# Substitution steps of a chunked scan moved one batch behind their loads, two buffers for the scan's loads, and a starting matrix that is loaded

## The chip, the cores and the metric

The kernel runs as one program on one core of a Trainium2 chip. The core has five engines that a trace names: PE (TensorE, the matmuls; PEld is its loading of weights), DVE (VectorE), ACT (ScalarE), POOL (GpSimd) and SP (SyncE, which here only issues DMAs). Each works through its own instructions strictly in order; they meet at semaphores. DMA transfers run beside them, started by an issue instruction on one of the engines' queues. The metric is the device time of one execution in microseconds (us).

## The reference

The reference runs two blocks one after the other. The first (a gated linear recurrence and dilated attention) is not touched. The second normalises and projects its input, feeds four branches (a pool mixer, a differential attention, a bidirectional RWKV scan and gates), merges them and ends with a mixture of experts. The change sits in the RWKV scan, which the reference writes as a step over tokens, 768 of them (256 of context and 512 latent), for two directions and 8 heads of 64:

```
def wkv_step(S, inp):
    r, w, k, v, a, b = inp
    sa = jnp.einsum('dbhvk,dbhk->dbhv', S, a)
    S = S * w[..., None, :] + sa[..., None] * b[..., None, :] + v[..., None] * k[..., None, :]
    return S, jnp.einsum('dbhvk,dbhk->dbhv', S, r)
```

## The kernel before

The scan is done in chunks of 64 tokens: 4 chunks of context and 8 latent ones, in each of two directions d, 24 in all. Two chunks make a batch; the 12 batches n = 0 to 11 alternate between the directions. Each batch has three functions:

- `ph_a`, once for each chunk: loads `kb` (b, k and decay of the chunk, 384 KB, L1133) and `kr`; four scans on DVE make the running sum of the decay, `cs` (L1143, L1145); ACT makes `ep` (L1147) and `em` (L1149), its exponentials with either sign; POOL and DVE scale `kr` by `ep` into the two halves of `AR` (L1153, L1155), POOL copies `dec` from `ep` (L1151), DVE scales b and k by `em` into `BK` (L1157). PE multiplies `BK` and `AR` (`pA`, L1163), DVE masks the product into `AMB` (L1167), and PE and ACT put a transpose of `BK` beside it (`ptb`, L1172, L1175).
- `ph_i`, once for each batch: the 32x32 blocks of `AMB` are stored to DRAM (`atD`, four DMAs, L1184) and loaded back as `LT`, 512 KB, the blocks repeated over partitions (L1187). `Ti`, the starting matrix, is copied from a constant by ACT (L1190). Then come 31 substitution steps of two small DVE instructions each (`Tm`, L1195, and `Ti`, L1197; 372 of each in all), which invert unit triangular blocks. Four DMAs store the result (`ttD`, L1200).
- `ph_b`, run by `run_b` for the batch two back: loads the inverse (`TT`, L1214) and the values (`XV`, `XW`), finishes the inverse with small matmuls `pi` and copies `T1` and `Qs` (L1246, L1247), makes `px` (L1269, copied to `XV` at L1272 and L1273), `pW` (L1283) and `WW` (DVE L1290 and L1292, ACT L1293), and carries the state `SI` over the chunks (`pch`, L1301 to L1313).

Between the batches the program is given other work of the second block, mainly projections with 512 KB weight loads (`wr`, L297; split by `wh` on ACT, L304, and `wl`, L305; matmuls `pf`) and the preparation of queries and keys.

No order is written out by hand. The program is built by a scheduler that simulates the engines with its own model of durations and, from the order of the code, the data and the free buffers, fixes one order for each engine's queue ahead of time. The tags that `w1` gives a tile have a number of buffers (`kb` 1, `ep` 2, `LT` 2, `Ti` 2, `AR` 6, `AMB` 3): an instruction that fills a buffer waits until the readers of what it held before are done, and what stands behind it on its queue waits with it. With one buffer, the load of `kb` for a chunk waits until `BK` of the chunk before has read it.

Of the kernel before, what the change touches and what calls it, by code (L numbers as in the profile page):

```python
# [12 lines left out]
AF = mybir.ActivationFunctionType  # L13
# [26 lines left out]
def _consts():  # L40
    f = np.float32
    groups, off = {g: [] for g in "012345"}, {}
    where = {"bias1": "1", "invf": "1", "cos2": "3", "sin2": "3", "hsel": "5", "hbc": "5",
             "mask": "2", "tinit": "2", "sgn": "2",
             "iota32": "4", "tokid": "4", "tri": "4", "slot": "4", "tokrow": "4"}

    def add(name, a):
        a = np.asarray(a, f)
        a = a.reshape(128, -1)
        g = where.get(name, "0")  # L50
        off[name] = (g, sum(p.shape[1] for p in groups[g]), a.shape[1])
        groups[g].append(a)

    p = np.arange(128)
    add("ident", np.eye(128))
    j = np.arange(512)
    d = p[:, None] - j[None, :] + 384
    n = ((d >= 0) & (d <= 128)).astype(int) + ((d >= 0) & (d % 4 == 0)) + ((d >= 0) & (d % 16 == 0))
    add("bias1", np.where(n > 0, np.log(np.maximum(n, 1).astype(np.float64)), NEG))
    add("invf", np.broadcast_to((10000.0 ** (-np.arange(32) / 32)).astype(f), (128, 32)))  # L60
    sel = np.zeros((128, 2))
    sel[0::32, 0] = 1
    sel[1::32, 1] = 1
    add("sel8", sel)
    add("ones", np.ones((128, 1)))
    add("nhalf", np.full((128, 8), -0.5))
    t = np.arange(512)
    inv16 = (10000.0 ** (-np.arange(16) / 16)).astype(f)
    ar = (t // 64).astype(f)[:, None] * inv16
    ac = (t % 64).astype(f)[:, None] * inv16  # L70
    cr, sr, c_, s_ = (fn(a.astype(np.float64)) for a in (ar, ac) for fn in (np.cos, np.sin))
    add("cos2", np.concatenate([cr, cr, c_, c_], 1).reshape(4, 128, 64).transpose(1, 0, 2))
    add("sin2", np.concatenate([-sr, sr, -s_, s_], 1).reshape(4, 128, 64).transpose(1, 0, 2))
    hs = np.zeros((128, 4, 8))
    hb = np.zeros((128, 4, 128))
    for ft in range(4):
        for e in range(2):
            hs[64 * e:64 * e + 64, ft, 2 * ft + e] = 1
            hb[2 * ft + e, ft, 64 * e:64 * e + 64] = 1
    add("hsel", hs)  # L80
    add("hbc", hb)
    b1 = np.zeros((128, 128))
    b1[:64, :64] = 1
    b1[64:, 64:] = 1
    add("bones", b1)
    add("iota32", np.broadcast_to(np.arange(32), (128, 32)))
    add("slot", np.broadcast_to(np.arange(64), (128, 64)))
    add("tokid", np.arange(512).reshape(4, 128).T)
    add("tokrow", np.broadcast_to(np.arange(512), (128, 512)))
    add("tri", p[:, None] < p[None, :])  # L90
    r = np.arange(64)

    m = np.zeros((128, 2, 2, 128))
    sg = np.ones((128, 2))
    for dd, (lt, le) in enumerate(((r[:, None] < r[None, :], r[:, None] <= r[None, :]),
                                   (r[:, None] > r[None, :], r[:, None] >= r[None, :]))):
        tr = np.concatenate([lt, le], 1)
        for e in range(2):
            m[64 * e:64 * e + 64, dd, e] = -0.5 * tr
            m[64 - 64 * e:128 - 64 * e, dd, e] = tr  # L100
    for e in range(2):
        sg[64 * e:64 * e + 64, e] = -0.5
    add("mask", m)
    add("sgn", sg)
    ti = np.zeros((4, 32, 8, 32))
    for g in range(4):
        for q in range(8):
            ti[g, :, q, 4 * q + g] = 1
    add("tinit", ti)
    return {"cst" + g: np.concatenate(v, 1) for g, v in groups.items()}, off  # L110


_CST, _COFF = _consts()
# [77 lines left out]
def _build(ctx, tc, A, out, dbg, upto):  # L191
    nc = tc.nc
    V, SC, GP, PE, SY = nc.vector, nc.scalar, nc.gpsimd, nc.tensor, nc.sync
# [87 lines left out]
    def cc(name):  # L281
        g, o, w = _COFF[name]
        return csts[g][:, o:o + w]
# [186 lines left out]
    for i in range(4):  # L470
        t = t2("x%d" % i, w=1024, tag="t4")
# [189 lines left out]
    for z, (ft, e) in enumerate(att):  # L661
# [6 lines left out]
        for j in range(4):  # L668
            pt = ps("pT", "aux")
            n = 512 - 128 * j  # L670
# [370 lines left out]
    for f in range(8):  # L1041
        src, g = (ya[f], vv("norm_rec")[:, f:f + 1]) if f < 4 else (yb[f - 4], vv("norm_att")[:, f - 4:f - 3])
# [52 lines left out]
    load_cst("2", cp2)  # L1095
    mask = cc("mask").rearrange("p (d e t) -> p d e t", d=2, e=2)
    sgn = cc("sgn")
    tinit = cc("tinit").rearrange("p (j t) -> p j t", j=8)
    ones64 = cc("ones")[:, 0:1].to_broadcast([128, 64])
    CW = 0.5 * math.exp(-0.5)  # L1100
    atD = [dp.tile([2, 2, 8, 32, 32], F32, name="atD%d" % i) for i in range(4)]
# [6 lines left out]
    def w1(name, shape=(4, 64), bufs=1, dt=F32):  # L1108
        p = rp if name == "AZ" else rpa if name in EARLY else rpb
        return p.tile([128] + list(shape), dt, tag=name, name=name, bufs=bufs)  # L1110
# [10 lines left out]
    for d in range(2):  # L1121
        for e in range(2):
            t = rp.tile([128, 4, 64], F32, name="SI%d%d" % (d, e))
# [5 lines left out]
    def ph_a(d, c, s, AMB):  # L1129

        lat = c >= 4
        kb = w1("kb", (3, 4, 64), 1)
        SY.dma_start(kb, kbD[lat][:, d, c - 4 * lat])  # L1133
        kr = w1("kr", (2, 4, 64), 2)
        SY.dma_start(kr[:, 0], kkD[:, c])
        if lat:
            SY.dma_start(kr[:, 1], rD[:, c])
        o0 = 1 - d
        cs = w1("cs", (4, 65))
        GP.memset(cs[:, :, 0:1] if d == 0 else cs[:, :, 64:65], 0.0)  # L1140
        for f in range(4):
            if d == 0:
                V.tensor_tensor_scan(cs[:, f, 1:65], ones64, kb[:, 2, f, :], 0.0, op0=ALU.add, op1=ALU.add)  # L1143
            else:
                V.tensor_tensor_scan(cs[:, f, 0:64][:, ::-1], ones64, kb[:, 2, f, ::-1], 0.0, op0=ALU.add, op1=ALU.add)  # L1145
        ep = w1("ep", (4, 65), 2)
        SC.activation(ep, cs, AF.Exp, scale=-CW)  # L1147
        em = w1("em")
        SC.activation(em, cs[:, :, o0:o0 + 64], AF.Exp, scale=CW)  # L1149
        dec = w1("dec", (4, 1), 7)  # L1150
        GP.tensor_copy(dec, ep[:, :, 64:65] if d == 0 else ep[:, :, 0:1])  # L1151
        AR = w1("AR", (4, 2, 64), 6)
        GP.tensor_tensor(AR[:, :, 0, :], kr[:, 0], ep[:, :, d:d + 64], ALU.mult)  # L1153
        if lat:
            V.tensor_tensor(AR[:, :, 1, :], kr[:, 1], ep[:, :, o0:o0 + 64], ALU.mult)  # L1155
        BK = w1("BK", (4, 2, 64), 2)
        V.tensor_tensor(BK.rearrange("p f a t -> p a f t"), kb[:, 0:2], bc(em[:, None], [128, 2, 4, 64]), ALU.mult)  # L1157

        nt = 128 if lat else 64
        pA = [ps("pA", "pa") for _ in par]  # L1160
        for f in range(4):
            for e, rows in par:
                PE.matmul(pA[e][:, nt * f:nt * (f + 1)],  # L1163
                          BK[rows, f].rearrange("p a t -> p (a t)"),
                          AR[rows, f, 0:nt // 64, :].rearrange("p a t -> p (a t)"), start=True, stop=True)
        for e in range(2):
            V.tensor_tensor(AMB[:, e, s, :, 0:nt], pA[e][:, 0:4 * nt].rearrange("p (f t) -> p f t", f=4),  # L1167
                            bc(mask[:, d, e, None, :nt], [128, 4, nt]), ALU.mult)
        pb = [ps("ptb", "pa") for _ in par]
        for f in range(4):  # L1170
            for e, rows in par:
                PE.transpose(pb[e][:, 64 * f:64 * f + 64],  # L1172
                             BK[rows, f].rearrange("p a t -> p (a t)"), ident[rows, rows])
        for e in range(2):
            SC.activation(AMB[:, e, s, :, 128:192], pb[e][:, 0:256].rearrange("p (f t) -> p f t", f=4),  # L1175
                          AF.Copy, scale=sgn[:, e:e + 1])
        return AR, dec

    def ph_i(d, AMB, bi):

        for e in range(2):
            for i in range(2):
# [3 lines left out]
        LT = w1("LT", (32, 32), 2)  # L1186
        SY.dma_start(LT.rearrange("p s t -> p (s t)"),  # L1187
                     atD[bi].rearrange("e i q s t -> (e i q) (s t)")[None].to_broadcast([4, 32, 1024]))
        T = w1("Ti", (8, 32), 2)
        SC.activation(T, tinit, AF.Copy)  # L1190
        tmp = w1("Tm", (8, 32))
        for s in (range(31) if d == 0 else range(31, 0, -1)):
            js, ts_ = (slice(0, s // 4 + 1), slice(s + 1, 32)) if d == 0 else (slice(s // 4, 8), slice(0, s))
# [8 lines left out]
    def ph_b(d, chs, sts, AMB, bi):  # L1202
# [3 lines left out]
        T = TT[d]  # L1206
# [33 lines left out]
        q2 = [slice(64 * e + 32 - 32 * d, 64 * e + 64 - 32 * d) for e in range(2)]  # L1240
        c1, c2 = slice(32 * d, 32 * d + 32), slice(32 - 32 * d, 64 - 32 * d)
        pi = ps("pi", "aux")
        T1, Qs = w1("T1", (2, 4, 32)), w1("Qs", (2, 4, 32))

        def evac(dst, src_):
            V.tensor_copy(dst[0], src_[0])  # L1246
# [71 lines left out]

    order = ([0, 1, 2, 3] + list(range(4, 12)), [3, 2, 1, 0] + list(range(11, 3, -1)))
    batches = [(d, order[d][2 * b:2 * b + 2]) for b in range(6) for d in range(2)]  # L1320
    pend = []

    def run_b():
        n, sts = pend.pop(0)
# [7 lines left out]
    def batch(n):  # L1332
        d, chs = batches[n]
        AMB = w1("AMB", (2, 2, 4, 192), 3)
        sts = {c - min(chs): ph_a(d, c, c - min(chs), AMB) for c in chs}
        ph_i(d, AMB, n % 4)
        pend.append((n, (d, chs, sts, AMB, n % 4)))
        if len(pend) > 2:
            run_b()
# [42 lines left out]
        GP.memset(t, 0.0)  # L1382
    for n in range(4, 12):
        batch(n)
    while pend:
        run_b()
    if upto <= 2:
# [744 lines left out]
```

## Time and profile before

| | |
|---|---|
| Times of three runs | 1940.88, 1953.85, 1959.17 us; median 1953.85 us |
| The profiled execution | 1948.57 us, of which the span of the trace is 1946.8 us; mean granted PE clock 0.938 |
| Busy over the span | PE 1732.8 us (89%), DVE 1062.6 (55%), ACT 618.2 (32%), POOL 406.4 (21%) |
| From 480 to 1160 us (680 us), the batches of the scan with the work beside them | PE 593.8 us busy, DVE 471.3, ACT 238.3, POOL 102.2; DMA share 0.54 |
| From 1440 to 1946 us, the mixture of experts | DMA share 1.02, 374 GB/s; PE 493.3 us busy |

The profile names each instruction by engine, line and tile and says what ended the idle time ahead of it. Chunks are counted 0 to 23 below in the order in which they are worked on, batches 0 to 11; batch n has the chunks 2n and 2n+1. The chain of waits follows the work that ended last back from the end of the program; its pieces are times for which the end of the program waited on just that work.

### The profile page before, as it was taken

To read this page: it belongs to the slowest core of one execution; us is meant where nothing else is said; L and a number is where in the kernel's file an instruction comes from. 1 tells how busy PE (TensorE), PEld (TensorE's weight loads), DVE (VectorE), ACT (ScalarE), POOL (GpSimd) and SP (SyncE) were. 2 spreads that over 40 slices of the span, in tenths; PEclk is the share of its full clock that TensorE was granted. 3 is DMA by queue.
4 is the path that set the end of the run, shared out by engine and by line. 5 is a ranking of instruction groups with operands and counts; after the bars stand their busy time and mean duration, and the time that the engine had idled before them with its cause. 6 is when DMAs were issued, how large, how long until landed. Compare 5 with 4: busy or idle time off the path is not lost.

```text
span 1946.8 us, 31337 instructions
## 1 busy us (share of the span) xinstructions
PE 1732.8 (89%) x12309; PEld 1233.5 (63%) x12310; DVE 1062.6 (55%) x2417; ACT 618.2 (32%) x1164; POOL 406.4 (21%) x326
## 2 busy tenths in 40 slices
PE   6899997966888988978889986989979999999998
PEld 3874567963565777767768864777944545444544
DVE  4555686174479845767777744676342333332432
ACT  4224454453444232333333333443221111110110
POOL 2520337351004101111220013722211010100000
PEclk8999998988988997889989998989989999999999
DMA  8335622567647545445565346635449999999998
GB/s 294 108 112 207 215 76 90 171 217 223 173 128 194 148 141 115 138 93 142 140 147 144 108 160 210 234 122 177 186 165 386 386 386 386 386 387 387 386 386 288
DMA packets 275296, 415.90 MB, mean 214 GB/s; under 512 B 104876, under 2 KB 126408, under 8 KB 274888
## 3 DMA queue, kind: packets, MB, share of 16 engines
q1 hardware_dynamic: 246248, 383.44, 59.4%
q10 hardware_dynamic: 25568, 16.78, 2.8%
q0 software_dynamic: 3328, 13.63, 2.5%
q8 instruction: 98, 1.61, 0.3%
q14 instruction: 54, 0.44, 0.1%
HBM read 370.26 MB, written 43.53 MB: 213 GB/s over the span
## 4 chain that ended last, share of the span: by engine, by line
PE 43%; DVE 5%; DMA 5%; ACT 1%; issue 1%; SPq 0%; POOL 0%; ACTq 0%; DVEq 0%; POOLq 0%
PE ped L1976 6%; PE peg L1937 6%; PE peu L1944 6%; PE pcb L2008 3%; PE po L1799 2%; PE pg L1910 2%; DMA kb<-kbD 2%; PE pg L1911 2%; PE pW L1283 1%; PE pf L312 1%; PE pf L310 1%; PE pf L311 1%; PE pbr L310 1%; PE pbr L311 1%; PE pbr L312 1%; PE dpo L1683 1%
## 5 line engine op out<-in xcount | busy, mean ns | idle before, releaser
L305 POOL TENSOR_TENSOR wl<-wr,wh 128x1024 fp32r<-128x1024 f32 x72 | 181.3, 2528 | 306.6 <-ACT wh L304 300.2
L304 ACT ACTIVATE wh<-wr 128x1024 fp32r<-128x1024 f32 x125 | 131.7, 1055 | 172.7 <-PE pf L311 61.0
L310 PE MATMUL pf<-h2h,wh 128*128 128x512 f32 x344 | 144.5, 420 | 20.7 <-ACT mth L1348 14.4
L311 PE MATMUL pf<-h2l,wh 128*128 128x512 f32 x344 | 142.6, 415 | 0.0
L312 PE MATMUL pf<-h2h,wl 128*128 128x512 f32 x344 | 141.8, 412 | 0.0
L1982 POOL TENSOR_TENSOR yl<-ey,yh 128x512 fp32r<-128x512 f32 x30 | 38.4, 1280 | 464.6 <-ACT yh L1981 464.6
L1976 PE MATMUL ped<-wd,hid 128*64 128x512 f32 (+1 forms) x528 | 127.4, 585 | 0.7 <-ACT hid L1960 0.7
L1937 PE MATMUL peg<-wg,hTg 128*64 128x512 f32 x512 | 127.0, 597 | 0.0
L1944 PE MATMUL peu<-wu,hTg 128*64 128x512 f32 x512 | 125.2, 595 | 0.0
L1195 DVE TENSOR_TENSOR Tm<-LT,Ti 128x60 f32<-128x60 f32 (+24 forms) x372 | 87.5, 235 | 43.2 <-DMA LT<-atD 35.0
L2009 DVE TENSOR_TENSOR acc<-acc,pcb 128x512 f32<-128x512 f32 (+1 forms) x124 | 76.0, 665 | 49.1 <-PE pcb L2008 49.0
L310 PEld LDWEIGHTS pf<-h2h,wh 128*128 128x128 f32 x344 | 67.5, 196 | 40.7 <-ACT mth L1348 14.7
L1197 DVE TENSOR_TENSOR Ti<-Ti,Tm 128x60 f32<-128x60 f32 (+24 forms) x372 | 82.4, 221 | 8.4
L1976 PEld LDWEIGHTS ped<-wd,hid 128*64 128x64 f32 x528 | 39.6, 136 | 70.9 <-issue 67.1
L1944 PEld LDWEIGHTS peu<-wu,hTg 128*64 128x64 f32 x512 | 42.9, 137 | 65.4 <-issue 64.1
L305 DVE TENSOR_TENSOR wl<-wr,wh 128x1024 fp32r<-128x1024 f32 x53 | 65.1, 1228 | 32.3 <-ACT wh L304 32.0
L1937 PEld LDWEIGHTS peg<-wg,hTg 128*64 128x64 f32 x512 | 41.9, 137 | 60.9 <-issue 58.4
L311 PEld LDWEIGHTS pf<-h2l,wh 128*128 128x128 f32 x344 | 67.6, 196 | 18.1 <-issue 3.2
L312 PEld LDWEIGHTS pf<-h2h,wl 128*128 128x128 f32 x344 | 67.2, 195 | 17.4 <-issue 1.1
L1981 ACT ACTIVATE yh<-ey 128x512 fp32r<-128x512 f32 x30 | 18.9, 630 | 163.5 <-DVE ey L1980 90.0
L1914 ACT ACTIVATE hTg<-pg,sh,gs 128x128 f32<-128x128 f32 x64 | 28.2, 457 | 121.4 <-PE peu L1944 55.4
L1917 DVE TENSOR_SCALAR hTg<-pg,gs,sh 128x128 f32<-128x128 f32 x64 | 25.3, 408 | 75.0 <-PE peu L1944 38.4
(962 smaller groups left out, 4468.0 us busy)
## 6 DMA issues: line engine op xcount, KB each, us to landing
wg<-in_w_exp_gate_dram SPq DMA_DIRECT2D x64, 1024.0 KB
wu<-in_w_exp_up_dram SPq DMA_DIRECT2D x64, 1024.0 KB
wd<-in_w_exp_down_dram SPq DMA_DIRECT2D x62, 1024.0 KB
wr<-in_w_in_dram SPq DMA_DIRECT2D x97, 512.0 KB
kb<-kbD SPq DMA_DIRECT2D x24, 384.0 KB
wr<-in_w_out_dram SPq DMA_DIRECT2D x16, 512.0 KB
LT<-atD SPq DMA_DIRECT2D x12, 512.0 KB
thD<-mth ACTq DMA_DIRECT2D x24, 256.0 KB
```

What stands on the lines that cost most here:

```text
L304: SC.activation(hi, raw, AF.Copy)
L305: cur.get("lo", GP).tensor_tensor(lo, raw, hi.bitcast(F32), ALU.subtract)
L310: PE.matmul(p, ah, bh, start=start, stop=False)
L311: PE.matmul(p, ah, bl, start=False, stop=False)
L312: PE.matmul(p, al, bh, start=False, stop=stop)
L1195: V.tensor_tensor(tmp[:, :nj, :n], bc(LT[:, s, None, ts_], [128, nj, n]), bc(T[:, js, s:s + 1], [128, nj, n]), ALU.mult)
L1197: V.tensor_tensor(T[:, js, ts_], T[:, js, ts_], tmp[:, :nj, :n], ALU.add)
L1937: mm = PE.matmul(pg[64 * a:64 * a + 64, :], hT[:, k, 64 * a:64 * a + 64], gp[a][k // 4][:, k % 4, :], start=(k == 0), stop=(k == 7), tile_ ...
L1944: PE.matmul(pu[64 * a:64 * a + 64, :], hT[:, k, 64 * a:64 * a + 64], up[a][k // 4][:, k % 4, :], start=(k == 0), stop=(k == 7), tile_posit ...
L1976: PE.matmul(pd[64 * a:64 * a + 64, :], hid[:, m * k + 64 * a:m * k + 64 * a + 64], dn[q][a][:, k, 0:q1 - q0], start=(k == 0), stop=(k == 3 ...
L2008: PE.matmul(p, ohT[R, 128 * i:128 * (i + 1)], yy[R, qs], start=(z == 0), stop=(z == len(parts) - 1))
L2009: V.tensor_tensor(acc[i][:, qs], acc[i][:, qs], p, ALU.add)
```

## The change

Four edits:

1. `ph_i` now ends with the load of `LT` and returns it. The substitution steps and the store of their result stand in a new function `ph_s`, which `batch(n)` calls for batch n-1 after `ph_i` of batch n. For the last batch it is called behind the loop.
2. `kb` has two buffers.
3. The starting matrix is loaded by a DMA on SP (128 KB, from a kernel input of its own) in place of the copy on ACT; the constant is no longer kept in SBUF.
4. `ep` has one buffer in place of two, and `T1` and `Qs` share one tile.

```diff
@@ ph_a
-        kb = w1("kb", (3, 4, 64), 1)
+        kb = w1("kb", (3, 4, 64), 2)
...
-        ep = w1("ep", (4, 65), 2)
+        ep = w1("ep", (4, 65))
@@ ph_i
         SY.dma_start(LT.rearrange("p s t -> p (s t)"),
                      atD[bi].rearrange("e i q s t -> (e i q) (s t)")[None].to_broadcast([4, 32, 1024]))
+        return LT
+
+    def ph_s(d, LT, bi):
+
         T = w1("Ti", (8, 32), 2)
-        SC.activation(T, tinit, AF.Copy)
+        SY.dma_start(T.rearrange("p j t -> p (j t)"), A["tinit"])
         tmp = w1("Tm", (8, 32))
         for s in (range(31) if d == 0 else range(31, 0, -1)):
...
@@ ph_b
-        T1, Qs = w1("T1", (2, 4, 32)), w1("Qs", (2, 4, 32))
+        T1 = Qs = w1("T1", (2, 4, 32))
@@ batch
-    pend = []
+    pend, loops = [], []
...
-        ph_i(d, AMB, n % 4)
+        LT = ph_i(d, AMB, n % 4)
+        while loops:
+            ph_s(*loops.pop(0))
+        loops.append((d, LT, n % 4))
...
     for n in range(4, 12):
         batch(n)
+    ph_s(*loops.pop(0))
     while pend:
         run_b()
```

What the scheduler makes of it, at two places. The first is SP's queue where the loads of chunk 16 stand (batch 8's first; `kb_8037` before, `kb_7962` in the change); `atD2` and `LT` are the store and the load of batch 6. Before:

```order
L1133 DMA kb_7715<-kbD8_2114 128x768
L1184 DMA atD2_4506<-AMB_7300 32x8x32 x4
L1187 DMA LT_7397<-atD2_4506 128x1x1024
L297 DMA wr_10506<-in_w_in_2_dram 128x1024
L297 DMA wr_10676<-in_w_in_2_dram 128x1024
L1133 DMA kb_8037<-kbD8_2114 128x768
L297 DMA wr_10710<-in_w_in_2_dram 128x1024
```

In the change:

```order
L1133 DMA kb_7962<-kbD8_2114 128x768
L1441 DMA gk1_10195<-vFD_2118 128x512
L1184 DMA atD2_4506<-AMB_7227 32x8x32 x4
L1187 DMA LT_7324<-atD2_4506 128x1x1024
L1133 DMA kb_8008<-kbD8_2114 128x768
L298 DMA wr_10494<-in_w_in_2_dram 128x1024
L298 DMA wr_10664<-in_w_in_2_dram 128x1024
L298 DMA wr_10698<-in_w_in_2_dram 128x1024
L1204 DMA ttD1_4509<-Ti_7326 256x1x32 x4
L1218 DMA TT1_4519<-ttD1_4509 32x8x32 x4
L1194 DMA Ti_8060<-in_tinit_dram 128x256
```

The load of `kb` for chunk 16, which stood behind the load of `LT` and two weight loads, now stands ahead of the stores of `atD`; behind `LT` there is now the load for chunk 17, and the three weight loads follow it. The load of `Ti` stands behind the load of `TT`.

The second is DVE's queue where the scans of chunk 16 (`cs_8042` before, `cs_7967` in the change) stand among the substitution steps. Before:

```order
L1461 TENSOR_TENSOR dro_10385<-dro_10385,dra_10386 128x256
L1195 TENSOR_TENSOR Tm_7059<-LT_7055,Ti_7057 128x8x2
L1197 TENSOR_TENSOR Ti_7057<-Ti_7057,Tm_7059 128x8x2
L1143 SCALAR_TENSOR_TENSOR cs_8042<-cst0_75,kb_8037 128x64 x3
L1195 TENSOR_TENSOR Tm_7059<-LT_7055,Ti_7057 128x8
L1143 SCALAR_TENSOR_TENSOR cs_8042<-cst0_75,kb_8037 128x64
L305 TENSOR_TENSOR wl_10509<-wr_10506,wh_10508 128x1024
L1197 TENSOR_TENSOR Ti_7057<-Ti_7057,Tm_7059 128x8
L1195 TENSOR_TENSOR Tm_7401<-LT_7397,Ti_7399 128x31
```

In the change:

```order
L1199 TENSOR_TENSOR Tm_7695<-LT_7324,Ti_7693 128x2x25
L1294 TENSOR_TENSOR WW_7526<-pW_7517,cst0_75 64x4x64
L1296 TENSOR_TENSOR WW_7526<-pW_7517,AR_6563 64x4x64
L1201 TENSOR_TENSOR Ti_7693<-Ti_7693,Tm_7695 128x2x25
L1155 TENSOR_TENSOR AR_7612<-kr_7597,ep_7606 128x4x64
L1199 TENSOR_TENSOR Tm_7695<-LT_7324,Ti_7693 128x2x24
L1201 TENSOR_TENSOR Ti_7693<-Ti_7693,Tm_7695 128x2x24
L1199 TENSOR_TENSOR Tm_7695<-LT_7324,Ti_7693 128x3x23
L1201 TENSOR_TENSOR Ti_7693<-Ti_7693,Tm_7695 128x3x23
L1143 SCALAR_TENSOR_TENSOR cs_7967<-cst0_75,kb_7962 128x64 x2
L1199 TENSOR_TENSOR Tm_7695<-LT_7324,Ti_7693 128x3x22
L1143 SCALAR_TENSOR_TENSOR cs_7967<-cst0_75,kb_7962 128x64 x2
```

Before, the first scan stands 18 rows behind the `BK` that frees the one buffer of `kb`; in the change 79 rows behind the `BK` of chunk 14, and a few rows behind `WW` and `AR`. The steps of `LT_7324` begin 23 rows ahead of the scans; before, those of the same batch (`LT_7397`) begin right behind them.

## Rows read from the trace of the kernel before

**Rows 1.** Timeline of DVE (start us, us, engine, line, operation, idle before it).

```profile
865.09 0.66 DVE L1143 TENSOR_TENSOR_SCAN cs<-cst,kb 128x64 f32<-128x64 f32 x3 [8.56 <-DMA kb<-kbD]
...
892.60 0.66 DVE L1143 TENSOR_TENSOR_SCAN cs<-cst,kb 128x64 f32<-128x64 f32 x3 [0.82 <-DMA kb<-kbD]
...
907.15 0.84 DVE L1145 TENSOR_TENSOR_SCAN cs<-cst,kb 128x64 f32<-128x64 f32 x4 [7.45 <-DMA kb<-kbD]
```

**Rows 2.** Timeline of SP, which issues DMAs, same columns.

```profile
849.14 0.56 SPq L1187 DMA_DIRECT2D LT<-atD  x1
...
851.83 0.33 SPq L1133 DMA_DIRECT2D kb<-kbD  x1
...
888.44 0.32 SPq L1133 DMA_DIRECT2D kb<-kbD  x1
```

**Rows 3.** Waits of DVE, 700 to 1060 us (total us, times, longest us).

```profile
DVE cs L1143 <- DMA kb<-kbD: 19.0, 5, 8.6
DVE Tm L1195 <- DMA LT<-atD: 17.6, 3, 8.6
...
DVE cs L1145 <- DMA kb<-kbD: 9.4, 3, 7.4
```

**Rows 4.** Chain of waits, 849 to 1180 us: shares; start us, us, what.

```profile
by line: DMA kb<-kbD 10.4%; PE pW L1283 7.1%; PE pf L312 5.0%; PE pf L310 5.0%; PE pf L311 5.0%; DMA wr<-in_w_in_dram 3.9%; PE pA L1163 3.4%; DMA LT<-atD 3.2%; issue 2.7%; DMA yD<-yt 2.7%; PE pt L310 2.4%; DMA gy<-yD 2.3%; PE pt L312 2.3%; 
...
851.83 13.24 DMA kb<-kbD
...
895.92 11.14 DMA kb<-kbD
...
941.09 10.13 DMA kb<-kbD
```

**Rows 5.** Timeline of PE: the instructions behind its idle times.

```profile
767.91 1.09 PE L1269 MATMUL px<-AZ,TT 64*64 64x128 f32 x5 [6.22 <-DVE TT L1246]
...
868.98 2.08 PE L1283 MATMUL pW<-AMB,XV 128*128 128x128 f32 x8 [7.67 <-DVE XV L1272]
...
909.54 2.07 PE L1283 MATMUL pW<-AMB,XW 128*128 128x128 f32 x8 [4.97 <-ACT WW L1293]
...
952.84 0.66 PE L1472 MATMUL dqT<-cst,dro 128*128 128x128 f32 x4 [3.57 <-DVE gk L1434]
...
954.69 1.65 PE L1283 MATMUL pW<-AMB,XV 128*128 128x128 f32 x6 [1.19 <-DVE XV L1272]
...
1006.51 0.36 PE L1231 MATMUL pz<-XV,AMB 64*64 64x64 f32 x1 [8.68 <-ACT XW L1273]
```

**Rows 6.** Busy us (instructions) per engine, granted PE clock, by stretch.

```profile
core 0: us, PE busy (x) PEld busy (x) DVE busy (x) ACT busy (x) POOL busy (x), PEclk, DMA share, GB/s
867.90:874.80 6.90, 5.51 (x62) 4.90 (x63) 5.55 (x20) 3.07 (x6) 0.68 (x1) 0.67 0.48 115
908.90:915.70 6.80, 6.16 (x55) 5.63 (x56) 6.41 (x21) 2.46 (x5) 3.56 (x5) 0.67 0.33 82
...
1080.00:1120.00 40.00, 40.00 (x478) 33.11 (x473) 31.80 (x95) 15.77 (x27) 0.14 (x2) 1.00 0.41 116
```

**Rows 7.** The copy of the initial T, and its waits (us, times).

```profile
L1190 ACT ACTIVATE Ti<-cst x12: 400/417/420, 486.7 to 1051.5; 128x256 f32<-128x256 f32 x12
...
  DMA ttD<-Ti: 29.9, 8
```

**Rows 8.** Timeline of POOL: half of AR, and work of another branch.

```profile
873.97 0.68 POOL L1153 TENSOR_TENSOR AR<-kr,ep 128x256 f32<-128x256 f32 x1 [18.53 <-DVE WW L1292]
...
908.24 1.01 POOL L323 TENSOR_TENSOR dsr<-dsr,cst 128x4 f32<-128x4 f32 x1 [13.63 <-DVE dsr L322]
...
910.75 0.90 POOL L1454 TENSOR_TENSOR dro<-dk,cst 128x256 f32<-128x256 f32 x1
...
912.02 1.30 POOL L1423 TENSOR_TENSOR gk<-gk,gk 128x512 f32<-128x512 f32 x1 [0.27 <-issue]
```

**Rows 9.** Timeline of ACT: the row of ep.

```profile
911.17 0.42 ACT L1147 ACTIVATE ep<-cs 128x260 f32<-128x260 f32 x1 [0.30 <-DVE AR L1155]
```

More of the change, by code (lines that the diff above doesn't have):

```diff
@@ L43, in _consts @@
     where = {"bias1": "1", "invf": "1", "cos2": "3", "sin2": "3", "hsel": "5", "hbc": "5",
-             "mask": "2", "tinit": "2", "sgn": "2",
+             "mask": "2", "sgn": "2",
              "iota32": "4", "tokid": "4", "tri": "4", "slot": "4", "tokrow": "4"}
@@ L108, in _consts @@
             ti[g, :, q, 4 * q + g] = 1
-    add("tinit", ti)
-    return {"cst" + g: np.concatenate(v, 1) for g, v in groups.items()}, off
+    res = {"cst" + g: np.concatenate(v, 1) for g, v in groups.items()}
+    res["tinit"] = ti.reshape(128, 256).astype(f)
+    return res, off
 _CST, _COFF = _consts()
@@ L1097, in _build @@
     sgn = cc("sgn")
-    tinit = cc("tinit").rearrange("p (j t) -> p j t", j=8)
     ones64 = cc("ones")[:, 0:1].to_broadcast([128, 64])
```

## The prediction

> **What bounds the kernel now.** I read the chain of waits first, then the waits of DVE and PE in the stretch of the scan, then the queue of SP around the loads concerned. Over the whole span PE is busy 89% of the time, so what the change can give is bounded by PE's idle time in the scan. The chain of waits for 849 to 1180 us puts 10.4% of that time (331 us, so 34 us) on the load of `kb`, above any single line of PE; it lies in three pieces of 13.24, 11.14 and 10.13 us, the loads for chunks 16, 18 and 20 [rows 4]. Each is issued right behind a load of `LT`: at 851.83 us where `LT` went out at 849.14 [rows 2]. It lands 13.2 us later, and DVE stands 8.56 us at the scan that reads it [rows 1]. The load for chunk 17 was issued with no load of `LT` just ahead, at 888.44 us [rows 2]; it is read at 892.60, 4.2 us later, for a wait of 0.82 us [rows 1]. So an even chunk's load is slow because `LT` is in the DMA engines ahead of it, and late because with one buffer it is not issued until `BK` has read the chunk before.
>
> From 700 to 1060 us DVE waits 19.0 + 9.4 = 28.4 us on `kb` in eight places, and 17.6 us on `LT` in three [rows 3]. PE pays for three of the `kb` waits: 7.67 us (chunk 16, through the copy of `XV`), 4.97 us (chunk 18, through `WW`), and 3.57 and 1.19 us (chunk 20) [rows 5]. That is 17.4 us. The other `kb` waits are taken up by PE's queued projections. Behind the two longest idle times PE also runs slowly: the granted clock is 0.67 over 6.90 us and 0.67 over 6.80 us, a mix of the levels 1.2 and 2.4 GHz, against 1.00 in a stretch without idle time [rows 6].
>
> **Two buffers for `kb`** are the part I count. In the changed queue of SP the load for chunk 16 stands ahead of the stores of `atD` and of `LT`, so it can be expected to take about the 4.2 us of chunk 17. On DVE its scans stand 79 rows behind the `BK` that frees the buffer. With the mean duration that each line has in the trace those rows are 28.8 us of work (18 rows and 5.3 us before). For chunks 16 to 23 this cover is between 18.8 and 33.5 us, 3.6 to 6.1 us before; the slowest load shown took 13.24 us [rows 4], so these waits go. For chunks 10, 12 and 14 the cover is only 1.2, 2.9 and 4.5 us: short waits stay there, and PE lost nothing to `kb` there. The odd chunk's load now stands behind `LT`; its cover is 20 us or more. The first term is the 17.4 us of PE's idle time [rows 5].
>
> The second term is the clock: 0.33 x (6.90 + 6.80) = 4.5 us [rows 6], if PE without the idle time keeps 1.00. Together 21.9 us.
>
> The Trainium skill gives a price for such a load, on the page DMA: Bandwidth & Descriptors, section Anatomy of one DMA: about 2.0 us and the bytes over 436 KB per us; estimated by it, 384 KB take 2.9 us, and with that little to hide the two buffers would be worth some 3 x 2.9 = 9 us in place of 22. The trace has 4.2 us for a load almost alone and 10 to 13 behind `LT`, and the measurement decides.
>
> **Steps one batch later.** As written, the steps of a batch get the two `ph_a` of the next batch as cover for `LT`. But the order was the scheduler's before too, and it had already put the steps late: the first step of the 12 batches stands on DVE at rows 501, 614, 699, 810, 911, 1044, 1159, 1273, 1395, 1517, 1615, 1699, and in the change at 505, 617, 696, 814, 918, 1046, 1158, 1279, 1388, 1508, 1615, 1702. The work between the last mask of a batch and its first step is 3.5, 2.4 and 3.9 us for batches 0, 3 and 4 in the change (3.5, 2.9 and 4.1 before), and it is there that DVE waits on `LT`, up to 8.6 us [rows 3]. So I take nothing. The lower bound is nothing gained. The upper is that these waits do go, with what PE loses by one, 6.22 us [rows 5], and about as much for the others: 10 us. For batches 8 and 10 the cover falls from 22.3 and 15.2 to 12.7 and 10.6 us, about what a load behind others takes (10 to 13 us): 0 to 2 us lost.
>
> **Initial T by DMA.** Twelve copies on ACT of 417 ns go, 5.0 us, and with them ACT's 29.9 us of waiting on the store of `ttD` [rows 7]. ACT is not the bound there, and PE's waits on it are counted above: 0 taken, 2 us at most. SP gets twelve issues of a third to half a microsecond. Each stands behind a load of `TT`, which waits for a later store than it does; the matrix is first read a batch later, by 28 us of DVE work or more, against 13 us for the slowest, bigger load. On SP's queue they delay what is behind them by 12 x 0.5 = 6 us at worst; behind them stand loads of `kr` and values that are used later, so 0.
>
> **`ep` with one buffer** is the cost. Now `ep` of chunk c+1 waits for `AR` and `dec` of chunk c; `AR` waits for a free buffer until `WW` of an old chunk is done (18.53 us once [rows 8]); and the one buffer of `cs` makes the scans of c+2 wait for `ep` of c+1. So from `WW` there is a chain: `AR` on POOL 0.68 [rows 8], `ep` on ACT 0.42 [rows 9], and two or three hand-overs, together some 1.9 us. On DVE the scans stand 1.7 us of work behind that `WW` for even chunks and 2.8 or more for odd ones. Some 0.2 us each would be the cost; with POOL or ACT a little late, 0.5 us for 8 even chunks, of which PE sees half: 2 us. At least it is nothing, at most it is the fourth case below. The Trainium skill has a rule against this edit (Trainium Kernel Development and Optimization, section Best Practices: double-buffer so that transfers and work overlap), and it names loads; here the second buffer goes from a tile that ACT fills.
>
> **`T1` and `Qs` in one tile** hold different partitions, and the second is computed from the first: 0.
>
> The sum: 21.9 - 2 = 20 us. The profiled execution took 1948.6 us and would take 1928.6. It lies 5.3 us under the median of the three runs, 1953.85 us; against that median the forecast is **1934 us**.
>
> **The rivals.**
> - All of it (chance 0.14). The `kb` waits that PE did not pay for also put DVE ahead, the waits on `LT` shrink and the clock keeps up: 34 us of the chain [rows 4] and some 6 of `LT`, 40 us: 1914 us. For it: the chain counts 34, not 17. Against it: PE is busy 40.00 of 40 us from 1080 [rows 6], so DVE ahead buys nothing there.
> - Eaten by the next wait (0.22). The three weight loads now follow `LT` and another `kb`; where DVE waits no more on `kb`, it may wait on `wl`, as at 1006 us, where PE lost 8.68 us so [rows 5]. Two more of these cost 17 us of the 20: 1951 us.
> - Slower (0.14): `ep`. If work of another branch stands between `WW` and `AR` on POOL, 1.01 + 0.90 + 1.30 us as at 908 to 913 us [rows 8], the chain from `WW` to the scan is 3.2 + 0.68 + 0.42 = 4.3 us against 1.7 of cover: 2.6 us for each of the 16 latent chunks, 42 us, less the 22: 1974 us. It decides from 22/16 = 1.4 us a chunk. For it: no slack at all in the order. Against it: in the changed order of POOL no such work stands right behind a `WW` whose `AR` is awaited, except ahead of chunk 14.
>
> **How the numbers follow.** The forecast has 0.50, with a range of its own of 1926 to 1942. The range of 8 in 10 leaves out the slower case and the edges: **1908 to 1965 us**. A measurement of this kernel can tell about 1%, 19.5 us, from no change: faster is below 1934.3, slower above 1973.4. The forecast lies on the first edge; 0.28 of it and the 0.14 of the first rival are faster, 0.42. The rest of it, 0.22, with the second rival's 0.22 and 0.02 of the last, are 0.46 within 1%. Slower are 0.12.
>
> **What would show it.** In the profile after, the loads of `kb` for chunks 16, 18 and 20 should be issued ahead of `LT` and be gone from the chain; DVE's waits on `kb` should fall from 28 us to under 8, PE's idle times of 7.67 and 4.97 us should be gone, and the granted clock of 840 to 960 us should rise towards 1.00. DVE's waits on `LT` for batches 3 and 4 should stand as before. The prediction is wrong if `cs` waits on ACT's `ep` by more than a microsecond a chunk, if `wl` waits grow by what `kb` waits lose, or if the waits on `LT` go too.

## The result, and the profile after

The changed kernel takes 1925.83 us (median of 4 runs, 1922.05 to 1934.39) against 1956.51 us (4 runs) of the kernel before beside it: a ratio of 0.9857, 95% interval 0.9818 to 0.9896, so 1.4% or about 28 us faster. A second comparison on another chip (e11 below) gave 0.9872 (0.9841 to 0.9903), about 25 us. The profiled execution took 1925.13 us, 23.4 us less than the one of before, which lies 8 us under its median.

Where the time came from is seen by cutting both profiles where PE has done about the same share of its work. Busy time of each engine, granted PE clock, DMA share and GB/s of the stretches, of the kernel before:

```profile
core 0: us, PE busy (x) PEld busy (x) DVE busy (x) ACT busy (x) POOL busy (x), PEclk, DMA share, GB/s
480.00:767.00 287.00, 241.55 (x1648) 182.90 (x1648) 180.94 (x450) 103.80 (x170) 43.97 (x64) 0.89 0.59 155
767.00:1162.00 395.00, 353.63 (x3930) 302.94 (x3930) 291.18 (x919) 134.88 (x264) 58.27 (x85) 0.93 0.50 130
1162.00:1441.00 279.00, 231.58 (x1378) 195.61 (x1380) 158.47 (x278) 105.20 (x201) 98.15 (x59) 0.91 0.51 179
1441.00:1946.00 505.00, 492.34 (x2573) 238.78 (x2571) 163.66 (x309) 63.93 (x121) 38.39 (x30) 1.00 1.02 375
```

and of the changed one:

```profile
core 0: us, PE busy (x) PEld busy (x) DVE busy (x) ACT busy (x) POOL busy (x), PEclk, DMA share, GB/s
477.00:759.00 282.00, 245.51 (x1707) 183.87 (x1707) 184.88 (x458) 104.00 (x168) 43.07 (x65) 0.90 0.60 160
759.00:1138.00 379.00, 354.83 (x3871) 302.66 (x3871) 289.51 (x912) 131.51 (x253) 54.48 (x85) 0.93 0.53 137
1138.00:1417.00 279.00, 232.17 (x1370) 196.31 (x1371) 157.72 (x278) 104.34 (x201) 97.84 (x59) 0.91 0.52 179
1417.00:1923.00 506.00, 490.98 (x2580) 236.93 (x2579) 163.43 (x309) 64.23 (x122) 38.34 (x30) 1.00 1.02 374
```

The stretch of batches 4 to 11, where the forecast was made, went from 395 to 379 us: 16 us. PE's idle time in it fell from 41.4 to 24.2 us. The early batches gave 5 us, 287 to 282. The border between the two is soft by some 4 us: up to it PE has done 59 more matmuls in the change (1707 against 1648 from the first cut on), 4 us of its busy time. Both stretches together hold the same 5578 matmuls; there PE's busy time rose from 595.2 to 600.3 us and its idle time fell from 86.8 to 60.7. The stretches behind the scan are as long as before. The 3 us left are from ahead of 477 us, where the change moves no work of the scan; other kernels of this study stand between 1 us later and 8 us earlier there.

A measure without that border is the length of the scan, from SP's first load of `kb` to DVE's last update of the state `SI`: 680.9 us before (480.32 to 1161.24) and 660.3 in the change (477.35 to 1137.62). So 20.6 of the 23.4 us are in the scan.

The places that the prediction named, in the changed kernel. The load of `kb` for chunk 16 and the load of `LT` on SP (columns as in [rows 2]):

```profile
820.21 0.33 SPq L1133 DMA_DIRECT2D kb<-kbD  x1
...
827.23 0.56 SPq L1187 DMA_DIRECT2D LT<-atD  x1
831.71 0.35 SPq L1133 DMA_DIRECT2D kb<-kbD  x1
```

and on DVE the scans of chunks 16 and 17:

```profile
852.37 0.47 DVE L1143 TENSOR_TENSOR_SCAN cs<-cst,kb 128x64 f32<-128x64 f32 x2
...
852.87 0.47 DVE L1143 TENSOR_TENSOR_SCAN cs<-cst,kb 128x64 f32<-128x64 f32 x2
...
863.26 0.83 DVE L1143 TENSOR_TENSOR_SCAN cs<-cst,kb 128x64 f32<-128x64 f32 x4
```

The load went out at 820.21 us, 7 us ahead of `LT`, and the scans no longer wait for it; before it was the other way round, 2.7 us behind `LT` [rows 2], with a wait of 8.56 us [rows 1]. The loads for chunks 18, 20 and 22 stand ahead of `LT` too, by 6 to 7 us (867.05, 906.19 and 951.70 us against 874.32, 913.42 and 957.67). Waits of DVE from 700 to 1060 us, answering to [rows 3]:

```profile
DVE Tm L1199 <- DMA LT<-atD: 24.5, 4, 9.6
DVE wl L306 <- ACT wh L305: 13.4, 6, 6.8
...
DVE AR L1155 <- ACT ep L1147: 3.1, 2, 2.3
...
DVE cs L1143 <- DMA kb<-kbD: 1.3, 1, 1.3
...
DVE cs L1145 <- DMA kb<-kbD: 0.8, 1, 0.8
```

The waits on `kb` fell from 28.4 to 2.1 us. Those on `LT` rose from 17.6 to 24.5: at the first steps of batches 3 and 4 they are 9.65 and 7.78 us, where they were 8.63 and 8.50, and at those of batches 8 and 10, whose cover the prediction had seen shrink, 3.79 and 3.30, where they were nothing and 0.50. The one of batch 8:

```profile
924.35 0.19 DVE L1199 TENSOR_TENSOR Tm<-LT,Ti 128x31 f32<-128x31 f32 x1 [3.79 <-DMA LT<-atD]
```

The idle times of PE that are left, answering to [rows 5]:

```profile
760.97 1.33 PE L1287 MATMUL pW<-AMB,XV 128*128 128x64 f32 x5 [4.83 <-ACT WW L1297]
...
926.08 1.34 PE L1287 MATMUL pW<-AMB,XV 128*128 128x128 f32 x8 [2.70 <-ACT WW L1297]
...
936.43 0.24 PE L1255 MATMUL pi<-cst,TT 32*32 32x32 f32 x2 [4.31 <-DMA TT<-ttD]
...
977.77 0.37 PE L1235 MATMUL pz<-XV,AMB 64*64 64x64 f32 x1 [5.02 <-ACT XW L1277]
```

The 7.67 us (chunk 16), 4.97 (chunk 18), 3.57 and 1.19 (chunk 20) are gone, and the 8.68 on `XW` [rows 5] is now 5.02. One of 2.70 us is new, beside the wait of batch 8's first step, and one of 4.31 us, on the load of `TT`. SP's queue shows why:

```profile
913.42 0.56 SPq L1187 DMA_DIRECT2D LT<-atD  x1
...
924.27 0.45 SPq L717 DMA_DIRECT2D KL<-dql  x1
...
929.32 2.58 SPq L1204 DMA_DIRECT2D ttD<-Ti  x4
...
933.44 0.81 SPq L1218 DMA_DIRECT2D TT<-ttD  x2
```

The steps whose result `ttD` stores were done at 920.6 us. SP stood still from 918.2 to 924.27 us, when `LT` had landed, then issued seven stores of another branch (`KL` and `KS`, to DRAM), and came to the store of `ttD` at 929.32, the load of `TT` behind it. The order fixed ahead of time has those transfers in front.

### The profile page after: what moved, and what is told of

It is laid out like the page before. It is cut to its first block, busy times and chain, and to the rows that moved or that the text cites. A ratio compares the mean times of both kernels' runs of the same rounds, so it can differ in the third digit from the quotient of the medians.

```text
span 1923.4 us, 31361 instructions
## 1 busy us (share of the span) xinstructions
PE 1738.0 (90%) x12309; PEld 1233.0 (64%) x12310; DVE 1063.5 (55%) x2417; ACT 614.3 (32%) x1152; POOL 401.3 (21%) x326
```

## Experiments

Each kernel was timed in five rounds beside the kernel before. Theory A is the prediction's: the second buffer of `kb` gives the gain. B holds that the later steps do, C that the copy taken from ACT does, D that with one `ep` buffer the scheduler puts the scans later and so hides the loads. The last column is the length of the scan in the one profiled execution, as above (680.9 us before); the two profiles of the change are 1.6 us apart in it.

| | us, median | ratio to before, 95% | scan, us |
|---|---|---|---|
| the change | 1925.83; 1926.78 | 0.9857 (0.9818 to 0.9896); 0.9872 (0.9841 to 0.9903) | 660.3; 658.7 |
| e1 steps back | 1937.37 | 0.9902 (0.9878 to 0.9926) | 674.3 |
| e2 one kb buffer | 1947.82 | 0.9964 (0.9948 to 0.9981) | 682.5 |
| e3 the room only | 1953.93 | 0.9992 (0.9971 to 1.0014) | 685.5 |
| e4 two ep buffers | 1924.99 | 0.9836 (0.9805 to 0.9866) | 664.5 |
| e5 steps only | 1950.16 | 0.9990 (0.9966 to 1.0013) | 684.1 |
| e6 decay split | 1922.17 | 0.9839 (0.9806 to 0.9872) | 661.8 |
| e7 split, steps later, T loaded | 1916.94 | 0.9813 (0.9780 to 0.9846) | 650.3 |
| e8 as e7, three decay buffers | 1915.65 | 0.9810 (0.9775 to 0.9845) | 652.7 |
| e9 as e7, LT in halves | 1884.35 | 0.9656 (0.9620 to 0.9692) | 622.0 |
| e10 split, steps later, T copied | 1911.22 | 0.9779 (0.9748 to 0.9811) | 648.7 |
| e12 LT in halves alone | 1935.97 | 0.9923 (0.9894 to 0.9951) | 668.3 |

**e1, the steps back in `ph_i`.**

```diff
-        return LT
-
-    def ph_s(d, LT, bi):
-
...
-        LT = ph_i(d, AMB, n % 4)
-        while loops:
-            ph_s(*loops.pop(0))
-        loops.append((d, LT, n % 4))
+        ph_i(d, AMB, n % 4)
...
-    ph_s(*loops.pop(0))
```

> The changed kernel with its substitution steps back in ph_i (two kb buffers, one ep buffer, T1 and Qs shared, initial T loaded). Theory A (the two kb buffers give the gain): 1922 to 1932 us, as the change. Rival B (the steps one batch later give it): 1945 to 1955 us. Rival C (the copy of the initial T gone from ACT gives it): as A.

1937.4 us, 5 us over A's range and 8 under B's. By the ratios 19 of the change's 28 us need no moved step; the rest, 6 to 9 us, may.

**e2, one `kb` buffer in the change.**

```diff
-        kb = w1("kb", (3, 4, 64), 2)
+        kb = w1("kb", (3, 4, 64), 1)
```

> The changed kernel with one kb buffer (steps one batch later, one ep buffer, T loaded). A: the waits of the scans on kb are back, 1945 to 1955 us. B: 1922 to 1932. C: 1922 to 1932. Rival D (with one ep buffer the scheduler puts the scans later on DVE: the work between the BK that frees kb and the scans of chunks 16, 18, 20, 22 is 20, 12, 8 and 16 us in this kernel, 5 in the one before): 1930 to 1940, DVE's waits on kb from 700 us on under 15 us in place of 28.

1947.8 us: A's number, 18 to 21 us of the change's gain gone by the ratios, and a scan no shorter than before; B and C are out as the main cause. But D's sign came true as well: the waits on `kb` from 700 us on are 12.4 us in place of 28.4, with little gain for it. From 840 to 1060 us, where 27.5 us were before, there are these:

```profile
DVE cs L1143 <- DMA kb<-kbD: 2.3, 1, 2.3
...
DVE cs L1145 <- DMA kb<-kbD: 0.5, 1, 0.5
```

PE still pays. The longest wait that is left, 9.44 us, is at the scan of chunk 14, with the copy of `XV` behind it on DVE, and PE, which needs that copy, stands 10.20 us:

```profile
816.10 0.66 DVE L1145 TENSOR_TENSOR_SCAN cs<-cst,kb 128x64 f32<-128x64 f32 x3 [9.44 <-DMA kb<-kbD]
```

```profile
818.26 1.12 PE L1287 MATMUL pW<-AMB,XV 128*128 128x64 f32 x4 [10.20 <-DVE XV L1276]
```

At chunk 16 DVE stands at another row instead, with the next copy of `XV` behind it, and PE 4.46 us:

```profile
863.75 1.23 DVE L306 TENSOR_TENSOR wl<-wr,wh 128x1024 fp32r<-128x1024 f32 x1 [8.74 <-ACT wh L305]
```

All waits of PE from 700 to 1060 us add up to 51.3 us before, 44.1 here, 52.2 in e3 (the next run) and 33.3 in the change.

**e3, only what makes the room** (the second buffer and the moved steps undone).

```diff
-        kb = w1("kb", (3, 4, 64), 2)
+        kb = w1("kb", (3, 4, 64), 1)
...
-        LT = ph_i(d, AMB, n % 4)
+        ph_i(d, AMB, n % 4)
...
```

> Only the edits that make room: one ep buffer, T1 and Qs in one tile, initial T loaded; one kb buffer, steps in ph_i. A and B: 1950 to 1958 us, or a few us slower. C: 1925 to 1935. D: 1930 to 1940, since the work ahead of the scans of chunks 16, 18, 20, 22 is 18, 13, 12 and 17 us.

1953.9 us, no difference. C and D fall. How the waits on `kb` can shrink for nothing is seen at chunk 16, in the rows of SP and of DVE:

```profile
842.01 0.47 SPq L1133 DMA_DIRECT2D kb<-kbD  x1
```

```profile
865.79 0.47 DVE L1143 TENSOR_TENSOR_SCAN cs<-cst,kb 128x64 f32<-128x64 f32 x2
```

The load goes out at 842.01 us, and the scans run at 865.79, 23.8 us later, without a wait. Before they ran at 865.09, after a wait of 8.56 us. To compare the two, a common mark is needed, since this trace is 7.9 us ahead where the scan begins. SP's first load of `kb`, here and before:

```profile
472.45 0.33 SPq L1133 DMA_DIRECT2D kb<-kbD  x1
```

```profile
480.32 0.33 SPq L1133 DMA_DIRECT2D kb<-kbD  x1
```

From that mark the scans of chunk 16 run after 384.8 us before, after 393.3 here, and after 375.0 in the change (852.37 from 477.35). The scheduler had put other work ahead of the scans, so the wait is not seen, but the scans are later, not earlier.

**e4, two `ep` buffers in the change** (a smaller `Tm` makes the room).

```diff
-        ep = w1("ep", (4, 65))
+        ep = w1("ep", (4, 65), 2)
...
-        tmp = w1("Tm", (8, 32))
+        tmp_ = w1("Tm", (80,))
...
```

> The changed kernel with two ep buffers (room for them from a smaller Tm, 80 in place of 256 elements a partition, with the same numbers computed). A: the small cost of the one buffer goes, 1920 to 1928 us. D: the scheduler pulls the scans forward again (2 to 6 us of work behind the BK that frees the buffer for 7 of the chunks 16 to 23's eight loads but two), so waits on kb come back: 1935 to 1950 us.

1925.0 us, against 1925.8 and 1926.8 of the change: by the medians the single buffer costs 1 to 2 us, by the ratios 4 to 7, and the intervals overlap. D's waits did not come back: DVE waits 5.0 us on `kb` from 700 us on.

**e5, the steps one batch later, alone** (the diff of e1 the other way round, on the kernel before).

> Only the steps one batch later; all else as in the kernel before (one kb buffer, two ep buffers, T copied by ACT). Theory A (the steps' move itself is worth nothing, the two runs with it were luckier orders): 1950 to 1958 us. Rival B2 (the move is worth the 5 to 9 us by which the kernels with it beat those without): 1943 to 1949 us.

1950.2 us, ratio 0.9990 (0.9966 to 1.0013): nothing that can be measured, though B2's range is not far. With the pairs e1 and the change (0.9902, 0.9857), e3 and e2 (0.9992, 0.9964), e6 and e10 (0.9839, 0.9779) the move gave 9, 5 and 12 us by the ratios, each at the edge of the intervals, all of one sign.

**e6, decay loaded apart.** The scans read only the third plane of `kb`. Here it is a tile of its own, with two buffers, and b and k keep one. The room comes from the smaller `Tm` of e4.

```diff
-        kb = w1("kb", (3, 4, 64), 1)
-        SY.dma_start(kb, kbD[lat][:, d, c - 4 * lat])
+        kb = w1("kb", (2, 4, 64), 1)
+        kd = w1("kd", (4, 64), 2)
+        SY.dma_start(kd, kbD[lat][:, d, c - 4 * lat, 2])
+        SY.dma_start(kb, kbD[lat][:, d, c - 4 * lat, 0:2])
...
```

> The kernel before with decay (128 KB) loaded apart from b and k (256 KB): two buffers for decay, still one for b and k; a smaller Tm makes the room; nothing else changed. The order has the decay of an even chunk ahead of the load of LT. Theory A (the scans' wait for a load that stands behind LT is what cost): 1927 to 1938 us, DVE's waits of the scans from 700 us under 8 us. Rival (it was not the scans' wait but the room or order that the other edits gave): 1948 to 1958 us, or slower by the 24 more issues on SP.

1922.2 us: with 1 KB more per partition and no edit to `ep`, `T1` or the place of the steps, it gives as much as the change or a little more. The smaller `Tm` does not make the steps themselves faster: their two instructions take 232 and 226 ns in the mean, 235 and 221 before. No scan waits for a load anywhere. What DVE waits on from 480 to 1110 us, of the kernel before:

```profile
DVE Tm L1195 <- DMA LT<-atD: 35.0, 5, 13.1
DVE wl L305 <- ACT wh L304: 27.1, 12, 7.7
DVE cs L1145 <- DMA kb<-kbD: 26.9, 7, 7.9
DVE cs L1143 <- DMA kb<-kbD: 23.0, 7, 8.6
```

and of e6:

```profile
DVE Tm L1198 <- DMA LT<-atD: 56.1, 9, 9.0
...
DVE wl L305 <- ACT wh L304: 12.3, 10, 2.6
```

The 49.9 us on `kb` are gone, early batches included, and 21 us of them have come back as waits on `LT`, 35.0 to 56.1.

**e7 and e8, the split with the steps later and T loaded; e8 with three decay buffers** (and, for their room, the smaller `Tm`, which e7 does not have).

```diff
-        kd = w1("kd", (4, 64), 2)
+        kd = w1("kd", (4, 64), 3)
```

> As the decay split, with the steps one batch later and the initial T loaded; two ep buffers, T1 and Qs apart. A with B2: 1918 to 1928 us, at the change or a few us under it. A alone: 1925 to 1935.

> As the run before it, with three buffers for decay. If what is left of the waits on early chunks' decay counts: 3 to 8 us under the run before it. If they are covered anyway: the same within 4 us.

1916.9 and 1915.7 us: some 10 us under the change by the medians, though the intervals of the ratios overlap; a third buffer gives nothing that can be measured. What is left is `LT`, 60.7 us of waiting in e7:

```profile
DVE Tm L1201 <- DMA LT<-atD: 60.7, 9, 9.0
```

**e9, `LT` in two tiles.** The steps go through the rows of `LT` one after the other, upwards or downwards, so half of it is enough to begin.

```diff
-        LT = w1("LT", (32, 32), 2)
-        SY.dma_start(LT.rearrange("p s t -> p (s t)"),
-                     atD[bi].rearrange("e i q s t -> (e i q) (s t)")[None].to_broadcast([4, 32, 1024]))
+        LT = [w1("LT%d" % h, (16, 32), 2) for h in range(2)]
+        for h in ((0, 1) if d == 0 else (1, 0)):
+            SY.dma_start(LT[h].rearrange("p s t -> p (s t)"),
+                         atD[bi][:, :, :, 16 * h:16 * h + 16].rearrange("e i q s t -> (e i q) (s t)")[None]
+                         .to_broadcast([4, 32, 512]))
...
```

> The decay split with the steps later and T loaded, and LT in two tiles of 256 KB, the half that the first steps read loaded first. DVE waits on LT for 61 us there in nine places. If these waits are the next thing that bounds the scan: 8 to 20 us under the kernel with one LT (1917), 1897 to 1909 us. If PE's own work bounds it by now, or the halves land together: 1912 to 1920 us.

1884.4 us, more than the 8 to 20 us expected: 33 us under e7 by the medians, 31 by the ratios, with a scan 28 us shorter, and 3.4% under the kernel before. The waits on `LT` fell from 60.7 us to

```profile
DVE Tm L1203 <- DMA LT<-atD: 13.7, 4, 4.6
```

For batch 0 the issue and the first step of e7 are

```profile
511.88 0.61 SPq L1189 DMA_DIRECT2D LT<-atD  x1
```

```profile
525.32 0.19 DVE L1201 TENSOR_TENSOR Tm<-LT,Ti 128x31 f32<-128x31 f32 x1 [8.72 <-DMA LT<-atD]
```

and of e9

```profile
506.29 1.93 SPq L1190 DMA_DIRECT2D LT<-atD  x2
```

```profile
513.85 0.19 DVE L1203 TENSOR_TENSOR Tm<-LT,Ti 128x31 f32<-128x31 f32 x1 [2.82 <-DMA LT<-atD]
```

From the issue to the first step it is 13.4 us with one load of 512 KB and 7.6 us where the first of two loads of 256 KB is enough. The order around it differs too, so not all of the 33 us is shown to be this.

**e10, the split with the steps later and T copied by ACT.** Against e6 only the steps have moved. Against e7 the load of T is gone, and `Tm` is the smaller one.

```diff
-        SY.dma_start(T.rearrange("p j t -> p (j t)"), A["tinit"])
+        SC.activation(T, tinit, AF.Copy)
```

> The decay split with the steps one batch later and T still copied by ACT: with the decay split alone (1922 us) this has only the move of the steps between them, with the run that also loads T (1917) only the load. If the move of the steps is worth what stood between these two: 1914 to 1919 us. If it is worth nothing and the load of T is: 1920 to 1926.

1911.2 us, under both ranges. By the ratios 0.9779 against 0.9813 of e7 the load of T is no gain over the copy, and perhaps a loss of some 6 us; the intervals overlap.

**e11, the change again.**

> The change itself again, beside the two above on the same chip: 1922 to 1932 us; with the decay split below it by 3 to 12 us.

1926.8 us, as the first time.

**e12, `LT` in halves alone**, on the kernel before; the diff of e9.

> The kernel before with LT in two tiles of 256 KB, the half that the first steps read loaded first, and nothing else changed. If the waits on LT cost by themselves what the two halves gave behind the decay split (1917 to 1884 us, 33 us): 1918 to 1930 us. If they cost only once the scans no longer wait on kb (an even chunk's load stands behind both halves as before): 1938 to 1952 us.

1936.0 us, ratio 0.9923, about 15 us: between the two expectations. Its waits on `kb` stayed:

```profile
DVE Tm L1197 <- DMA LT<-atD: 30.1, 6, 9.7
DVE cs L1145 <- DMA kb<-kbD: 29.6, 9, 6.4
DVE cs L1143 <- DMA kb<-kbD: 23.0, 9, 8.4
```

Behind the split (e7 to e9) the same edit gave 33 us. That the two waits hide a part of each other's cost fits this, but is not shown: e9 also has the later steps and the loaded T, and no run puts the halves on the split alone.

## Why the prediction was right, and where its terms were off

The forecast was 1934 us, 20 us faster; it came out at 1926, some 28 us by the first comparison and 25 by the second, at the lower edge of the forecast's own range of 1926 to 1942. The step it rested on holds: with `kb` alone taken back (e2) 18 to 21 us of the gain are gone, and the room alone (e3) or the moved steps alone (e5) give nothing. That the sum came so near is in part luck: the clock's 4.5 us did not come, and the early batches and the moved steps, both taken as 0, gave some 5 and 6 to 9 us.

- **PE's idle time, 17.4 us: right.** The three named idle times are gone; in the stretch of batches 4 to 11 PE's idle time fell by 17.2 us, net of new ones. That these two numbers meet is luck too: other idle times got shorter, as the 8.68 us that is now 5.02, and new ones of 2.70 and 4.31 us came. The price was read from PE, not from DVE's 28.4 us of waiting nor from the chain's 34 us, and that was the right row: the first rival (40 us) did not come.
- **The clock, 4.5 us: wrong.** The granted clock of that stretch is 0.93 before and after, and PE's busy time for the same 5578 matmuls did not fall (595.2 to 600.3 us). From 840 to 960 us the clock rose from 0.91 to 0.94, not to 1.00; from 867 to 907 us it is 1.00, from 907 to 947, where the new idle times are, 0.83.
- **One `ep` buffer, 2 us: not to be told from nothing** (e4). DVE waits for `ep` 3.1 us in two places. The fourth case did not come.
- **Steps one batch later, taken as 0: too little, within its bound of 10.** Alone it gives nothing; in this kernel it is 6 to 9 us (e1), 5 to 12 by all three pairs. By what it gains is open: DVE waits no less on `LT` with it (24.5 us from 700 us on, e1 17.2). The loss that the prediction saw for batches 8 and 10, 0 to 2 us, came as waits of 3.79 and 3.30 us on DVE.
- **Initial T by DMA, 0: right that it is no gain** (e3, e10).
- **The early batches, taken as 0: 5 us.** There the waits on `kb` went only from 21.7 to 16.6 us, since the second buffer is freed by `BK`, which is late there: two loads go out at 553.76 and 563.32 us, just when a `BK` ends (553.73 and 563.29), and the scan that reads the second waits 7.65 us.
- **The rival of the next wait** came in part, and not where it looked. DVE's waits on `wl` for ACT went only from 11.3 to 13.4 us, and PE's 8.68 us became 5.02. Waits on `LT` grew from 17.6 to 24.5 us, and PE's on `TT` from 2.4 to 9.0, of which 4.31 us stem from SP's standstill and order. They took a part, not 17 of the 20 us as its price had it.
- **Why the even chunks' loads were slow: argued more than shown.** The load for chunk 18 stands right behind `LT` and took 11.14 us [rows 4], but between `LT` and the load for chunk 16 there are two weight loads, and one ahead of that for chunk 20. The price that the prediction quotes from the Trainium skill (DMA: Bandwidth & Descriptors, Anatomy of one DMA) is the page's fit for transfers issued by GpSimd; these loads are issued by SP, and the sum does not use it.

What the prediction passed over is the size of the buffer. It priced the second buffer as the change has it, 3 KB per partition, with a chain of edits to make room. e6 shows that the buffer was not held for the sake of what the scans read: decay's third is free as soon as the scans have run, while b and k are kept until `BK`. The other thing passed over is that `LT`, whose waits it took as staying, was the larger bound behind `kb`: 33 us of e9, not all of them shown to be its waits.

## What to carry to other kernels

Where a tile is loaded in one piece but read by two users at different times, split it by user before giving it a second buffer: here a third of the memory gave at least as much. Where a loop walks through a loaded tile in order, load it in pieces in that order, so that the first piece starts the loop. A wait that disappears from the trace is a gain only if the instruction now runs earlier: compare its start, from a mark that both traces have, and the waits of the engine whose idle time is the price, not the wait that is gone.

## What the runs showed of the hardware

One thing was unexpected: on SP an issue of another branch's store stood still for 6.1 us until the load of `LT` had landed, though it needs nothing of it:

```profile
SPq L717 <- DMA LT<-atD: 6.1, 1, 6.1
```

The second profile of the change has it at the same line (6.0 us), and all traces of this study have such standstills, at other lines; in the kernel before a load of `XV` stood 6.5 us. Where `LT` comes in halves of 256 KB none is longer than 3.1 us (e9). Whether that is a limit on transfers under way or a semaphore that the trace puts down to the wrong event stays open.

Another is how little runs while such a load comes in. In the kernel before, from 858.80 to 864.30 us, just before the load for chunk 16 lands at 865.07, the 16 DMA engines are busy for a quarter of their time (columns as in the first table):

```profile
858.80:864.30 5.50, 2.52 (x54) 2.38 (x52) 0.00 (x0) 1.35 (x2) 0.00 (x0) 1.00 0.26 88
```

That is 88 GB/s, where the mixture of experts has 375. So at its end the wait is not for the bandwidth of all 16. Which transfer and which engines are busy then the trace does not tell, and no run lays out `LT` or its load in another way; the halves of e9 are the only edit to it.
